# Separate places for the casts and subtractions of the sums and of w_down's parts in the seven-product scheme

## The chip, the cores and the metric

The kernel runs on one core of one Trainium2 chip. The metric is the device time of one execution in microseconds (us). The kernel before takes 2257.21 us, the median of three runs (2255.51 to 2260.72).

## What is computed

The reference is one layer of a streaming encoder on 2048 prompt rows and 64 sample rows of 1024 features. The change lies in its last part, the feed-forward network:

```python
def _post(x, mix, ln1_g, ln1_b, w_gate_up, w_down, ln2_g, ln2_b):
    h = _layernorm(ALPHA * x + mix, ln1_g, ln1_b)
    gu = h @ w_gate_up
    f = (jax.nn.silu(gu[..., :D_FF]) * gu[..., D_FF:]) @ w_down
    return _layernorm(ALPHA * h + f, ln2_g, ln2_b)
```

D_FF is 2816, so w_down is 2816 x 1024. All values are fp32. A matrix product is made of three fp32r products: each operand is held as a high part (a cast) and a low part (the operand minus its high part), and high by high, high by low and low by high are summed in PSUM.

## The kernel before, in words

The rows are worked on in four blocks b (576, 512, 512 and 512 rows). Within a block the 2816 columns of the gate and up matrices come in 22 slices i of 128. The two matrices of a slice are multiplied with the block's h by a scheme of seven smaller products (`product`, numbered 1 to 7), each 12 matmuls of 256 columns in blocks 1 to 3. The list `order` is the order of all these products: for slice i it is 1, then 4 and 3 of the slice before, then 5, 6, 2, 7. So a slice takes seven places of the list and a pair of slices c = (2c, 2c+1) takes 14.

For w_down, blocks 1 to 3 use a second scheme of seven products on most pairs: c = 2 to 9 in blocks 1 and 2, c = 2 to 8 in block 3, 23 pairs in all (`strassen`). One product of a pair is two units (`unit`, u = 0 and 1), each three matmuls of 512 columns (lines 1321 to 1323) into a PSUM bank and one addition by VectorE (DVE) of the bank to y (line 1326). The left operands are g, the gated activations, or sums and differences of g; the right ones are parts of w_down, or differences that were stored in DRAM as wt_d.

The order around the change is written by hand. The last loop goes through `order`; at each place it records first the weights' forms for five places later (`make`), then the product, then what `at(place, ...)` has put there, in the order in which it was put. p0 is the place of product 3 of slice 2c+1; "place n" below means p0 + n, and place 14 is place 0 of the next pair. Each engine does its own instructions strictly in the recorded order. At place 0 the second half of g of the pair's second slice is ready (line 917). Then `put_f` splits it (ScalarE, ACT, casts at line 112; DVE subtracts at line 113), and `f_sums` makes four sums on GpSimd (POOL, line 879) and splits each, all at place 0. The units stand at places 0 to 13; product 2's two units (places 1 and 3) both use bank S0, so the unit at place 3 needs the addition of the one at place 1.

The parts of w_down are loaded (`load_f`, DMA from the SP queue, three buffers "draw"), and split two to six places later by `split_f` (ACT line 112, DVE line 113, five buffers "wd"). POOL, besides, makes the low part of the gate weights' forms 1 and 2 (line 113, wf), each after an ACT cast.

Of the kernel before, what the change touches and what calls it, by code (L numbers as in the profile page):

```python
# [8 lines left out]
F32 = mybir.dt.float32  # L9
F32R = mybir.dt.float32r  # L10
AF = mybir.ActivationFunctionType
ALU = mybir.AluOpType
# [4 lines left out]
P = 128  # L17
# [28 lines left out]
def hybrid_step(ctx: ExitStack, tc: tile.TileContext, x_prompt, x_sample, xT_prompt, xT_sample, cache_kT, cache_v, w_in,  # L46
                ln_v_g, ln_v_b, sinks, w_spatialT, vecs, w_out, w_gate_up, w_down, ln2_g, ln2_b, rope,
                y_prompt, y_sample, wk_p, wv_p, nk_s, nv_s, nvm_s):
    nc = tc.nc
# [61 lines left out]
    def split(hi, lo, src, on=None):  # L111
        nc.scalar.copy(hi, src)  # L112
        (on or nc.vector).tensor_tensor(out=lo, in0=src, in1=hi.bitcast(F32), op=ALU.subtract)  # L113
# [727 lines left out]
            nc.gpsimd.tensor_tensor(out=src, in0=gu_src[b, i][2], in1=src, op=ALU.subtract)  # L841

    ff, acc, part, banks = {}, {}, {}, {}
    ffs, spare, g_t = {}, [], {}

    def bank(name):

# [4 lines left out]
    def half_form():  # L852

        if not spare:
            f = f2.tile([P, 4 * NHX], F32R, name="ff", tag="ff", bufs=4)
            spare.extend(f[:, j * 2 * NHX:j * 2 * NHX + 512].rearrange("p (s t) -> p s t", s=2) for j in range(2))
        return spare.pop(0)
# [12 lines left out]
    def put_f(b, c, prod, src):  # L870
        f = ffs[b, c, prod] = half_form()
        split(f[:, 0], f[:, 1], src)

    def f_sums(b, c):

        x, y = g_t.pop((b, 2 * c)), g_t.pop((b, 2 * c + 1))
        for prod, o, a, d, op in ((5, y[:, 1], x[:, 1], y[:, 1], ALU.add), (7, x[:, 1], x[:, 0], x[:, 1], ALU.subtract),
                                  (6, x[:, 0], y[:, 1], x[:, 0], ALU.subtract), (3, y[:, 0], y[:, 0], x[:, 0], ALU.subtract)):
            nc.gpsimd.tensor_tensor(out=o, in0=a, in1=d, op=op)  # L879
        for prod, o in ((5, y[:, 1]), (6, x[:, 0]), (7, x[:, 1]), (3, y[:, 0])):  # L880
            put_f(b, c, prod, o)

    def tmp(name):
        if early:
# [366 lines left out]
    f2 = fl.enter_context(tc.tile_pool(name="f2", bufs=1, side="right"))  # L1251
# [56 lines left out]
                          w_down[(2 * c + x[0]) * P:(2 * c + x[0] + 1) * P, x[1] * 512:(x[1] + 1) * 512])  # L1308
        d_raw[b, c, "f", prod] = raw

    def split_f(b, c, prod):
        hl = f2.tile([P, 2, 512], F32R, name="wd", tag="wd", bufs=5)
        split(hl[:, 0], hl[:, 1], d_raw.pop((b, c, "f", prod)))
        wd[b, c, "f", prod] = hl

    def unit(b, c, prod, u):
        pd = bank({1: f"D{u}", 6: f"D{u}", 7: f"D{u}", 4: f"D{u}", 2: "S0"}.get(prod, f"S{1 - u}"))
        f, w = ffs[b, c, prod], wd[b, c, "f", prod]
        new = prod in (1, 2, 5)
        fh, fl = f[:, 0, u * P:u * P + P], f[:, 1, u * P:u * P + P]  # L1320
        nc.tensor.matmul(pd, fh, w[:, 0], start=new, stop=False, skip_group_check=not new)  # L1321
        nc.tensor.matmul(pd, fh, w[:, 1], start=False, stop=False, skip_group_check=not new)
        nc.tensor.matmul(pd, fl, w[:, 0], start=False, stop=True, skip_group_check=not new)  # L1323
        r, h = Y_OF[prod]
        y = y_t[TILES[b][2 * r + u]][:, h * 512:(h + 1) * 512]
        nc.vector.tensor_tensor(out=y, in0=pd, in1=y, op=ALU.add)  # L1326
# [104 lines left out]
    def at(pos, f):  # L1431
        todo.setdefault(pos, []).append(f)
# [8 lines left out]
    for b in range(NB):  # L1441
        first, last = b * NO, b == NB - 1
        for c in range(NFF // 2):
            p0 = start[b, 2 * c + 1, 3]
            d_load, d_split = (-8, -1, -5, -3), (-3, 5, -1, 4)
            if strassen(b, 2 * c):
                for prod, q0, q1 in ((1, -7, -3), (2, -6, -2), (6, -2, 2), (5, -1, 3), (3, 1, 5), (7, 3, 7), (4, 5, 9)):
                    at(p0 + q0, lambda b=b, c=c, prod=prod: load_f(b, c, prod))
                    at(p0 + q1, lambda b=b, c=c, prod=prod: split_f(b, c, prod))
                for q, prod, u in ((0, 1, 0), (1, 2, 0), (2, 1, 1), (3, 2, 1), (5, 6, 0), (6, 5, 0), (7, 5, 1), (8, 3, 0), (8, 6, 1),  # L1450
                                   (9, 3, 1), (10, 7, 0), (11, 7, 1), (12, 4, 0), (13, 4, 1)):
                    at(p0 + q, lambda b=b, c=c, prod=prod, u=u: unit(b, c, prod, u))
                continue
            if b == 0:
                d_load, d_split = (-6, -2, 8, 0), (1, 0, 10, 3)
                for j, q0, q1 in ((0, 2, 4), (1, 4, 6), (2, 5, 7), (3, 11, 13)):
                    at(p0 + q0, lambda c=c, j=j: w_sum(c, j))
                    at(p0 + q1, lambda c=c, j=j: w_store(c, j))
            elif c == 0:
                d_load, d_split = (-5, 1, -3, 2), (0, 6, 3, 7)  # L1460
            elif c == 1:
                d_load, d_split = (-8, -1, -4, 1), (-3, 5, 1, 6)
            elif c == NFF // 2 - 1 and not last:
                d_load, d_split = (0, 2, 1, 6), (5, 7, 6, 9)
            elif last and c == NFF // 2 - 2:
                d_load, d_split = (-7, -5, -6, -2), (-4, -2, -3, 2)
            if last and c == NFF // 2 - 1:
                d_load, d_split = (-14, -11, -13, -8), (-11, -3, -4, -2)
            for h in range(2):
                for i in (2 * c, 2 * c + 1):  # L1470
                    at(p0 + d_load[2 * (i % 2) + h], lambda b=b, i=i, h=h: load_d(b, i, h))
                    at(p0 + d_split[2 * (i % 2) + h], lambda b=b, i=i, h=h: split_d(b, i, h, b == NB - 1 and i > NFF - 3 and (i, h) != (NFF - 2, 0)))
            if c < NFF // 2 - (2 if last else 1):
                where = (5, 6, 7, 8, 9, 12, 13, 14, 15, 16) if b == 0 else (2, 4, 5, 7, 9, 10, 12, 13)
                if c == 0 and b:
                    where = (10, 12, 14, 16, 17, 18, 19, 19) if b == 1 else (6, 10, 12, 14, 15, 16, 17, 18)
                for k, (h, t) in enumerate((h, t) for h in (range(2) if b else (1, 0)) for t in TILES[b]):
                    at(p0 + where[k], lambda b=b, c=c, t=t, h=h: down(b, c, t, h))
            elif not last:
                new = list(TILES[b + 1])  # L1480
                if b:
                    at(p0 + 3, lambda t=new.pop(0): new_y(t))
                late = 0 if b else 2
                for k, t in enumerate(TILES[b]):
                    for h in range(2):
                        at(p0 + 10 + 2 * k + (h if b else 2 - h), lambda b=b, c=c, t=t, h=h: down(b, c, t, h))
                    steps = finish_steps(t)
                    for q, f in zip((11, 12, 13, 15, 17), steps):
                        at(p0 + 2 * k + q + late, f)
                    at(p0 + 2 * k + 20 + late, lambda t=new.pop(0): new_y(t)) if new else None  # L1490
        if not last:
            for pos, f in later_steps(b + 1):
                at(first + NO + pos, f)
# [104 lines left out]
```

## Time and profile before

| | |
|---|---|
| median of 3 runs | 2257.21 us (2255.51 to 2260.72) |
| the profiled execution | 2258.49 us, span 2256.3 us |
| busy: TensorE matmul (PE) | 2111.6 us, 94% |
| busy: DVE | 1613.2 us, 71% |
| busy: ACT | 1001.6 us, 44% |
| busy: POOL | 697.8 us, 31% |
| mean granted TensorE clock | 0.975 |

The share of busy time says which engine is loaded, not what it loses. For that one reads whom PE waited for, and then the instructions in order of time around such a wait. The granted clock is given as a share of full speed: 1.00 is 2.4 GHz, 0.50 is 1.2 GHz.

### The profile page before, as it was taken

The numbers are of one execution on the slowest core, as the hardware profiler recorded it, in microseconds if no ns is written. First come the engines' busy times: TensorE is split into PE (matmuls) and PEld (weight loads), VectorE is DVE, ScalarE is ACT, GpSimd is POOL, SyncE is SP. The second block draws the span as 40 slices with busy tenths as digits, with TensorE's granted clock in tenths as the row PEclk, the third lists the DMA queues.
The fourth block names the chain that finished last, engine by engine and source line by source line (L and its number), as shares of the span: only waits on it lengthen the run. The fifth ranks groups of instructions, "written<-read, shape, count | busy, mean of one in ns | idle before, by whom it ended". The sixth has DMA issues, their size and how long they took to land.

```text
span 2256.3 us, 36282 instructions
## 1 busy us (share of the span) xinstructions
PE 2111.6 (94%) x13081; PEld 1887.1 (84%) x13081; DVE 1613.2 (71%) x3176; ACT 1001.6 (44%) x2385; POOL 697.8 (31%) x644
## 2 busy tenths in 40 slices
PE   8999999989988999999999899999998999999997
PEld 6888888867767899899888888888888888988886
DVE  6877777786887767777785666677576668566665
ACT  6666666653444444444423334343333344334443
POOL 0222222121223667766411332221223212122220
PEclk9999999989999999999999999999999999999999
DMA  5111111144564767767875676777676667766663
GB/s 192 38 38 38 41 50 34 34 144 156 193 215 175 290 230 262 260 246 262 289 268 200 238 268 215 252 276 259 231 248 242 244 236 292 241 223 226 235 232 119
DMA packets 189155, 447.21 MB, mean 198 GB/s; under 512 B 22608, under 2 KB 53072, under 8 KB 188976
## 3 DMA queue, kind: packets, MB, share of 16 engines
q1 hardware_dynamic: 168432, 426.22, 53.8%
q10 hardware_dynamic: 20368, 18.35, 2.4%
q8 instruction: 103, 1.69, 0.3%
q14 instruction: 76, 0.62, 0.1%
q0 software_dynamic: 176, 0.33, 0.1%
HBM read 345.94 MB, written 98.89 MB: 197 GB/s over the span
## 4 chain that ended last, share of the span: by engine, by line
PE 59%; DVE 21%; ACT 6%; issue 5%; POOL 4%; DMA 4%; ACTq 0%; SPq 0%; DVEq 0%; POOLq 0%
PE bankA L900 5%; PE bankA L901 4%; PE bankA L902 4%; POOL g L879 2%; PE pj L158 2%; PE pj L159 2%; PE pj L160 2%; DVE ff L113 2%; PE po L160 2%; PE po L158 2%; PE po L159 2%; DVE y L1326 2%; PE pd L159 2%; PE bankC L901 2%; PE pd L160 2%
## 5 line engine op out<-in xcount | busy, mean ns | idle before, releaser
L113 POOL TENSOR_TENSOR wf<-guraw,wf 128x512 fp32r<-128x512 f32 x173 | 249.5, 1442 | 702.5 <-ACT wf L112 679.8
L900 PE MATMUL bankA<-hf,wf 128*128 128x256 f32 x1056 | 312.7, 296 | 14.9 <-ACT a L906 14.8
L901 PE MATMUL bankA<-hf,wf 128*128 128x256 f32 x1056 | 310.6, 294 | 0.0
L902 PE MATMUL bankA<-hf,wf 128*128 128x256 f32 x1056 | 310.4, 294 | 0.0
L113 DVE TENSOR_TENSOR wd<-draw,wd 128x512 fp32r<-128x512 f32 x245 | 183.1, 748 | 116.2 <-ACT wd L112 113.1
L900 PEld LDWEIGHTS bankA<-hf,wf 128*128 128x128 f32 x1056 | 213.5, 202 | 27.5 <-ACT a L906 18.3
L901 PEld LDWEIGHTS bankA<-hf,wf 128*128 128x128 f32 x1056 | 213.1, 202 | 9.4
L902 PEld LDWEIGHTS bankA<-hf,wf 128*128 128x128 f32 x1056 | 212.7, 201 | 0.0
L112 ACT CAST wf<-guraw 128x512 fp32r<-128x512 f32 x264 | 163.2, 618 | 15.9 <-DMA guraw<-in_w_gate_up_dram 8.7
L906 ACT COPY a<-bankA 128x256 f32<-128x256 f32 x198 | 73.3, 370 | 203.6 <-PE bankA L902 203.3
L901 PE MATMUL bankC<-hf,wf 128*128 128x256 f32 x528 | 149.3, 283 | 2.7 <-DVE hf L113 2.7
L112 ACT CAST wd<-draw 128x512 fp32r<-128x512 f32 x245 | 150.8, 616 | 1.5 <-PE bankD L160 0.8
L900 PE MATMUL bankC<-hf,wf 128*128 128x256 f32 x528 | 149.4, 283 | 0.0
L902 PE MATMUL bankC<-hf,wf 128*128 128x256 f32 x528 | 148.4, 281 | 0.0
L113 DVE TENSOR_TENSOR ff<-g,ff 128x256 fp32r<-128x256 f32 x161 | 80.2, 520 | 86.9 <-ACT ff L112 86.9
L1326 DVE TENSOR_TENSOR y<-bankD,y 128x512 f32<-128x512 f32 x184 | 125.8, 684 | 22.5 <-PE bankD L1323 22.5
L941 ACT ACTIVATE a<-a 128x256 f32<-128x256 f32 (+1 forms) x88 | 37.4, 425 | 226.2 <-DVE a L910 225.1
L112 ACT CAST ff<-g 128x256 fp32r<-128x256 f32 x161 | 63.2, 406 | 163.5 <-DVE g L917 101.2
L900 PE MATMUL accA<-hf,wf 128*128 128x288 f32 x352 | 105.0, 298 | 8.5 <-ACT a L906 4.9
L1321 PE MATMUL bankS<-wd,ff 128*128 128x512 f32 x138 | 58.4, 423 | 58.1 <-DVE y L1326 58.1
L901 PEld LDWEIGHTS bankC<-hf,wf 128*128 128x128 f32 x528 | 99.5, 188 | 8.7 <-DVE hf L113 3.2
L902 PE MATMUL accA<-hf,wf 128*128 128x288 f32 x352 | 104.0, 296 | 0.4 <-DVE wf L113 0.4
(332 smaller groups left out, 6592.1 us busy)
## 6 DMA issues: line engine op xcount, KB each, us to landing
wf<-wf_d SPq DMA_DIRECT2D x264, 512.0 KB, 5.1
guraw<-in_w_gate_up_dram SPq DMA_DIRECT2D x110, 512.0 KB, 6.2
wf_d<-wf SPq DMA_DIRECT2D x88, 512.0 KB, 4.8
draw<-in_w_down_dram SPq DMA_DIRECT2D x153, 256.0 KB, 4.0
draw<-wt_d SPq DMA_DIRECT2D x92, 256.0 KB, 5.5
guraw<-in_w_gate_up_dram SPq DMA_DIRECT2D x66, 256.0 KB, 6.5
wt_d<-draw SPq DMA_DIRECT2D x44, 256.0 KB, 3.3
hraw<-h_d SPq DMA_DIRECT2D x42, 256.0 KB, 5.7
```

The costliest lines, as they stand in the source:

```text
L112: nc.scalar.copy(hi, src)
L113: (on or nc.vector).tensor_tensor(out=lo, in0=src, in1=hi.bitcast(F32), op=ALU.subtract)
L158: nc.tensor.matmul(out, ah, bh, start=(i == 0), stop=False)
L159: nc.tensor.matmul(out, ah, bl, start=False, stop=False)
L160: nc.tensor.matmul(out, al, bh, start=False, stop=(i == n - 1))
L879: nc.gpsimd.tensor_tensor(out=o, in0=a, in1=d, op=op)
L900: nc.tensor.matmul(ps, wh, hh, start=(new and k == 0), stop=False, skip_group_check=not new)
L901: nc.tensor.matmul(ps, wh, hl, start=False, stop=False, skip_group_check=not new)
L902: nc.tensor.matmul(ps, wl, hh, start=False, stop=(k == 3), skip_group_check=not new)
L906: nc.scalar.copy(part[i, key][:, :n], ps)
L1321: nc.tensor.matmul(pd, fh, w[:, 0], start=new, stop=False, skip_group_check=not new)
L1326: nc.vector.tensor_tensor(out=y, in0=pd, in1=y, op=ALU.add)
```

## The change

Three things change for the 23 pairs. `f_sums` keeps the four sums on POOL at place 0, but their casts and subtractions are no longer made there: for the sums of products 5, 6, 3 and 7 the cast (`put_hi`) is at places 3, 4, 5, 6 and the subtraction (`put_lo`) one place later. The split of w_down's parts becomes a cast (`split_hi`) and, one place later, a subtraction (`split_lo`). Products 5 and 6 change places (the units at 5 and 6), with their loads and splits, and four of the loads are one place later.

```diff
+            f_sum[b, c, prod] = o
-            put_f(b, c, prod, o)
+    def put_hi(b, c, prod):
+        ffs[b, c, prod] = half_form()
+        nc.scalar.copy(ffs[b, c, prod][:, 0], f_sum[b, c, prod])
+    def put_lo(b, c, prod):
+        f = ffs[b, c, prod]
+        nc.vector.tensor_tensor(out=f[:, 1], in0=f_sum.pop((b, c, prod)), in1=f[:, 0].bitcast(F32), op=ALU.subtract)
...
-                for prod, q0, q1 in ((1, -7, -3), (2, -6, -2), (6, -2, 2), (5, -1, 3), (3, 1, 5), (7, 3, 7), (4, 5, 9)):
+                for prod, q0, q1 in ((1, -6, -3), (2, -5, -2), (5, -2, 2), (6, -1, 3), (3, 1, 5), (7, 4, 7), (4, 6, 9)):
                     at(p0 + q0, lambda b=b, c=c, prod=prod: load_f(b, c, prod))
-                    at(p0 + q1, lambda b=b, c=c, prod=prod: split_f(b, c, prod))
+                    at(p0 + q1, lambda b=b, c=c, prod=prod: split_hi(b, c, prod))
+                    at(p0 + q1 + 1, lambda b=b, c=c, prod=prod: split_lo(b, c, prod))
...
+                for q, prod in ((3, 5), (4, 6), (5, 3), (6, 7)):
+                    at(p0 + q, lambda b=b, c=c, prod=prod: put_hi(b, c, prod))
+                    at(p0 + q + 1, lambda b=b, c=c, prod=prod: put_lo(b, c, prod))
```

What stands in a row on DVE around place 0, before. The names: a is a partial result of a gate product, g the gated activations and their sums, ff the split form of either, wf a form of the gate weights, wd the split part of w_down, y the output rows; bankS_12902 is bank S0.

```order
L910 TENSOR_TENSOR a_14932<-bankC_12337,a_14932 128x256
L917 TENSOR_TENSOR g<-a_14979,a_14932 128x256
L113 TENSOR_TENSOR ff<-g,ff 128x256 x5
L1326 TENSOR_TENSOR y<-bankD_12798,y 128x512
L113 TENSOR_TENSOR wf<-guraw,wf 128x512
L1326 TENSOR_TENSOR y<-bankS_12902,y 128x512
L113 TENSOR_TENSOR wd<-draw,wd 128x512
L1326 TENSOR_TENSOR y<-bankD_12852,y 128x512
L910 TENSOR_TENSOR a_15004<-bankS_12228,a_15004 128x256
```

The same stretch on DVE after the change, from place 0 to the subtraction of product 5's sum at place 4 and the first addition of product 5 (bankS_12228 is bank S1):

```order
L926 TENSOR_TENSOR g<-a_14979,a_14930 128x256
L113 TENSOR_TENSOR ff<-g,ff 128x256
L1338 TENSOR_TENSOR y<-bankD_12798,y 128x512
L113 TENSOR_TENSOR wf<-guraw,wf 128x512
L1338 TENSOR_TENSOR y<-bankS_12902,y 128x512
L1338 TENSOR_TENSOR y<-bankD_12852,y 128x512
L919 TENSOR_TENSOR a_15003<-bankS_12228,a_15003 128x256
L1326 TENSOR_TENSOR wd<-draw,wd 128x512
L1338 TENSOR_TENSOR y<-bankS_12902,y 128x512
L946 TENSOR_TENSOR a_15154<-bankC_12168,a_15154 128x256
L1326 TENSOR_TENSOR wd<-draw,wd 128x512
L890 TENSOR_TENSOR ff<-g,ff 128x256
```

Four of the five ff subtractions have left the head of this stretch; the first of them now stands at its end, behind line 946 and a wd subtraction.

On ACT, before, at places 0 to 5 of a pair:

```order
L112 CAST ff<-g 128x256 x5
L112 CAST wf<-guraw 128x512
L906 COPY a_14763<-bankA_12134 128x256
L112 CAST wd<-draw 128x512
L941 ACTIVATE a_14654<-a_14654 128x256
L112 CAST wd<-draw 128x512
L906 COPY a_14815<-bankA_12134 128x256
L112 CAST wf<-guraw 128x512
```

On ACT, after, for the same places:

```order
L112 CAST ff<-g 128x256
L112 CAST wf<-guraw 128x512
L915 COPY a_14753<-bankA_12134 128x256
L1322 CAST wd<-draw 128x512
L950 ACTIVATE a_14653<-a_14653 128x256
L1322 CAST wd<-draw 128x512
L886 CAST ff<-g 128x256
L915 COPY a_14803<-bankA_12134 128x256
L886 CAST ff<-g 128x256
L112 CAST wf<-guraw 128x512
```

At place 4 a cast of a sum (line 886) has come between the copy of product 7 (line 915) and the cast of form 2 (line 112), whose low part POOL makes.

## Rows read from the trace of the kernel before

**Rows 1.** PE's waits: what was waited for, us in total, times, longest.
```profile
PE bankS L1321 <- DVE y L1326: 58.1, 25, 5.7
```

**Rows 2.** Stretches: length, each engine's busy time (instructions), granted clock, DMA share, GB/s.
```profile
1213.00:1490.40 277.40, 253.94 (x1681) 235.33 (x1680) 184.23 (x326) 108.65 (x245) 78.97 (x72) 0.94 0.69 240
1592.30:1866.50 274.20, 250.97 (x1682) 232.38 (x1681) 184.43 (x326) 108.75 (x245) 79.04 (x72) 0.96 0.69 242
1968.40:2200.50 232.10, 217.78 (x1472) 202.61 (x1471) 151.84 (x282) 93.52 (x212) 60.16 (x56) 0.96 0.65 227
1357.30:1389.40 32.10, 30.05 (x213) 27.92 (x211) 21.54 (x41) 13.38 (x30) 8.61 (x9) 1.00 0.69 237
1389.40:1423.00 33.60, 31.56 (x213) 29.31 (x211) 21.54 (x40) 13.29 (x30) 8.59 (x9) 0.95 0.65 228
1479.50:1484.00 4.50, 3.30 (x22) 2.69 (x21) 4.50 (x7) 1.41 (x3) 0.89 (x1) 1.00 0.41 106
```

**Rows 3.** Timeline at places 0 to 3 of a pair: start, us, instruction [idle before <-releaser].
```profile
1391.40 0.43 DVE L113 TENSOR_TENSOR ff<-g,ff 128x256 fp32r<-128x256 f32 x1 [0.47 <-ACT ff L112]
...
1391.91 3.27 POOL L879 TENSOR_TENSOR g<-g 128x256 f32<-128x256 f32 x4 [1.69 <-DVE ff L113]
...
1394.83 1.30 DVE L113 TENSOR_TENSOR ff<-g,ff 128x256 fp32r<-128x256 f32 x3 [1.08 <-ACT ff L112]
...
1396.05 0.68 DVE L1326 TENSOR_TENSOR y<-bankD,y 128x512 f32<-128x512 f32 x1
...
1396.65 0.68 DVE L113 TENSOR_TENSOR wf<-guraw,wf 128x512 fp32r<-128x512 f32 x1
1397.25 0.68 DVE L1326 TENSOR_TENSOR y<-bankS,y 128x512 f32<-128x512 f32 x1
...
1397.98 0.50 PE L1321 MATMUL bankS<-wd,ff 128*128 128x512 f32 x1 [2.04 <-DVE y L1326]
```

**Rows 4.** Timeline at places 11 and 12 of the same pair, around product 7's end.
```profile
1416.62 0.39 PE L1321 MATMUL bankD<-wd,ff 128*128 128x512 f32 x1
...
1416.82 0.37 ACT L906 COPY a<-bankA 128x256 f32<-128x256 f32 x1 [1.25 <-PE bankA L902]
...
1417.09 0.40 PE L1323 MATMUL bankD<-wd,ff 128*128 128x512 f32 x1
...
1417.09 0.62 ACT L112 CAST wd<-draw 128x512 fp32r<-128x512 f32 x1
...
1417.23 0.42 DVE L937 TENSOR_TENSOR a<-bankC,a 128x256 f32<-128x256 f32 x1 [1.15 <-ACT a L906]
...
1417.57 0.68 DVE L1326 TENSOR_TENSOR y<-bankD,y 128x512 f32<-128x512 f32 x1
...
1417.61 0.62 ACT L112 CAST wf<-guraw 128x512 fp32r<-128x512 f32 x1
...
1418.16 0.68 DVE L113 TENSOR_TENSOR wd<-draw,wd 128x512 fp32r<-128x512 f32 x1
...
1418.31 1.69 POOL L113 TENSOR_TENSOR wf<-guraw,wf 128x512 fp32r<-128x512 f32 x1 [10.08 <-ACT wf L112]
...
1418.74 0.40 PE L1321 MATMUL bankD<-wd,ff 128*128 128x512 f32 x1
```

**Rows 5.** Timeline where ACT casts a sum and then a form (place 13).
```profile
1387.93 0.41 ACT L112 CAST ff<-g 128x256 fp32r<-128x256 f32 x1 [1.69 <-DVE g L917]
1388.24 0.62 ACT L112 CAST wf<-guraw 128x512 fp32r<-128x512 f32 x1
```

**Rows 6.** Timeline where DVE and POOL both read SBUF.
```profile
1269.72 1.48 POOL L747 TENSOR_TENSOR hraw<-hraw,hsum 128x512 f32<-128x512 f32 x1
...
1269.97 1.78 DVE L113 TENSOR_TENSOR wd<-draw,wd 128x512 fp32r<-128x512 f32 x1
```

**Rows 7.** A unit's last matmul and its weight load: duration ns min/median/max, span, form.
```profile
L1323 PEld LDWEIGHTS bankD<-wd,ff x184: 187/187/188, 1214.6 to 2200.0; 128*128 128x128 f32 x184
```

**Rows 8.** Loads of w_down's parts (line 1307): time from issue to landing.
```profile
DMA to landing us min/median/max: 2.5/4.3/8.8
```

More of the change, by code (lines that the diff above doesn't have):

```diff
@@ L843, in hybrid_step @@
     ff, acc, part, banks = {}, {}, {}, {}
-    ffs, spare, g_t = {}, [], {}
+    ffs, spare, g_t, f_sum = {}, [], {}, {}
     def bank(name):
@@ L1309, in load_f, with split_hi, split_lo @@
         d_raw[b, c, "f", prod] = raw
[L1311 to L1314, printed above, removed]
+    def split_hi(b, c, prod):
+        hl = wd[b, c, "f", prod] = f2.tile([P, 2, 512], F32R, name="wd", tag="wd", bufs=5)
+        nc.scalar.copy(hl[:, 0], d_raw[b, c, "f", prod])
+    def split_lo(b, c, prod):
+        hl = wd[b, c, "f", prod]
+        nc.vector.tensor_tensor(out=hl[:, 1], in0=d_raw.pop((b, c, "f", prod)), in1=hl[:, 0].bitcast(F32), op=ALU.subtract)
     def unit(b, c, prod, u):
@@ L1446, in hybrid_step @@
             if strassen(b, 2 * c):
-                for prod, q0, q1 in ((1, -7, -3), (2, -6, -2), (6, -2, 2), (5, -1, 3), (3, 1, 5), (7, 3, 7), (4, 5, 9)):
+                for prod, q0, q1 in ((1, -6, -3), (2, -5, -2), (5, -2, 2), (6, -1, 3), (3, 1, 5), (7, 4, 7), (4, 6, 9)):
                     at(p0 + q0, lambda b=b, c=c, prod=prod: load_f(b, c, prod))
-                    at(p0 + q1, lambda b=b, c=c, prod=prod: split_f(b, c, prod))
-                for q, prod, u in ((0, 1, 0), (1, 2, 0), (2, 1, 1), (3, 2, 1), (5, 6, 0), (6, 5, 0), (7, 5, 1), (8, 3, 0), (8, 6, 1),
+                    at(p0 + q1, lambda b=b, c=c, prod=prod: split_hi(b, c, prod))
+                    at(p0 + q1 + 1, lambda b=b, c=c, prod=prod: split_lo(b, c, prod))
+                for q, prod, u in ((0, 1, 0), (1, 2, 0), (2, 1, 1), (3, 2, 1), (5, 5, 0), (6, 6, 0), (7, 5, 1), (8, 3, 0), (8, 6, 1),
                                    (9, 3, 1), (10, 7, 0), (11, 7, 1), (12, 4, 0), (13, 4, 1)):
                     at(p0 + q, lambda b=b, c=c, prod=prod, u=u: unit(b, c, prod, u))
+                for q, prod in ((3, 5), (4, 6), (5, 3), (6, 7)):
+                    at(p0 + q, lambda b=b, c=c, prod=prod: put_hi(b, c, prod))
+                    at(p0 + q + 1, lambda b=b, c=c, prod=prod: put_lo(b, c, prod))
                 continue
```

## The prediction

> **What bounds the kernel now.** PE is busy nearly all the time, so I first read whom it waited for. One row stands out: a unit into bank S waited for DVE's addition to y, 58.1 us in 25 waits [rows 1]. The second view is the table of stretches [rows 2]. Its first three rows are the three stretches with the 23 pairs of the seven-product scheme, 277.4 + 274.2 + 232.1 = 783.7 us. A place with one unit takes 2.12 us, from one unit's start to the next (1416.62 to 1418.74) [rows 4], so a pair without waits would take 14 x 2.12 = 29.7 us and 23 of them 683 us. About 101 us are lost there. The table also shows the granted clock at 0.94, 0.96 and 0.96 in these stretches: some of the time is spent at 1.2 GHz instead of 2.4, which costs 277.4 x 0.06 + 274.2 x 0.04 + 232.1 x 0.04 = 37 us. A pair whose clock stayed at 1.00 takes 32.1 us, one with a drop 33.6 (fourth and fifth row) [rows 2]: 2.4 us of waiting, and 1.5 us more where the clock fell.
>
> The third view, the order of time at places 0 to 3, says where the wait comes from [rows 3]. DVE subtracts the first ff at 1391.40. It then stands at the head of four more, each of which needs an ACT cast of a sum that POOL is still making (four sums, 3.27 us from 1391.91). The last three end at 1396.13. Behind them are queued two additions to y and one weight subtraction; the addition from bank S0, whose unit had long ended, starts only at 1397.25 and ends at 1397.93, and PE, after 2.04 us of idling, starts the unit of place 3 at 1397.98.
>
> **Part one, the sums' splits leave place 0.** No instruction is removed or added; 23 x 4 casts and 23 x 4 subtractions move. DVE's queue at place 0 is then the ff subtraction (2.00 us after the unit of place 0 starts, at 1389.40), an addition, a weight subtraction and the addition from S0. With the spacing of 0.60 us from one 512-wide operation to the next [rows 3] they start at 2.34, 2.94 and 3.54 and the last ends at 4.2. The unit of place 3 is due at 3 x 2.13 = 6.4. Even if the weight subtraction, now beside POOL's sums, takes 1.78 us as one does beside POOL [rows 6], the addition ends at 5.4. So this wait goes, and with it the drop of the clock that follows. Worth: 58.1 us of waits plus 37 us of clock, 95 us, less 3 us that I leave off, because two of the 25 waits must be at other places (there are 23 pairs) and because the half clock costs nothing where it falls into a wait: 92 us. The stretches' lengths allow 101 at most.
>
> **Part two, the first subtraction that is now due late.** What is late next? I walked the new order from place 0 with the rows' spacings, looking for each unit at when its operands are ready. One place comes out short: the third matmul of product 5's first unit (place 5), which needs the subtraction put at place 4. Count from the end of product 7 (place 4), as which the end of the same product at 1416.62 can stand [rows 4]. ACT's copy starts at 0.20 and DVE's addition of line 937 at 0.61. The next DVE instruction starts 0.34 later, at 0.95; it is now a wd subtraction. The ff subtraction stands behind it, 0.60 later, at 1.55, and takes 0.43 [rows 3]: 1.98. PE meanwhile does product 1, 1.42 us (1417.32 to 1418.74 at this spot, a place less a unit of 0.70), and two matmuls, 0.47 (1416.62 to 1417.09) [rows 4]: the third is due at 1.89, and its weights must be loaded first (0.19 us) [rows 7]. Undisturbed, that is a wait of about 0.3 us a pair.
>
> But POOL is there at the same moment. After the copy ACT's next cast starts 0.27 later, at 0.47 [rows 4]; it is now a sum's cast, and the form's cast follows 0.31 later [rows 5], at 0.78, takes 0.62, and POOL starts 0.08 after its end (1418.23 to 1418.31) [rows 4], at 1.48. What two engines reading SBUF do to each other can be seen [rows 6]: a wd subtraction of 0.68 us that started 0.25 us after a POOL subtraction took 1.78, ending 0.55 us after POOL's end; it was held until POOL was done. The other way round POOL's subtraction came 0.15 us after a DVE one and took 1.69 us where the one on its own takes 1.29 (1.69 less the 0.40 for which DVE held it) [rows 4]. So DVE's wd subtraction holds POOL until about 0.95 + 0.55 = 1.50, POOL gets its turn there, before the ff subtraction at 1.55, and keeps it until 2.79; the ff subtraction then needs some 0.28 more, as its 0.43 less the start-up that passes while it is held, and ends at 3.07. With 0.05 for the signal (1397.93 to 1397.98) [rows 3] and the weight load the third matmul starts at 3.3 instead of 1.89: 1.4 us a pair, 32 us in 23 pairs. The margin is thin, 0.05 to 0.07 us, between POOL's 1.48 to 1.50 and DVE's 1.55; I take the collision, because in all my sums POOL comes first, and keep the other end, 7 us, for the range.
>
> **Part three, w_down's casts and subtractions a place apart.** DVE no longer stands waiting for ACT between the two. That time is off PE's path once part one has emptied the queue; I cost it at nothing, and the later subtraction of each part (half a place to a place before its unit) has at least 1 us in hand in my walk, but for bank S1 at place 10, where the addition of product 3's unit ends only some 0.2 us before product 2 needs the bank. If that fails it costs tenths of a us. The loads of four parts have three places, 6.4 us, instead of four until their cast; the median landing is 4.3 us, the longest 8.8 [rows 8]. The loads are issued as soon as their buffer is free, mostly 7 us or more before the cast by my walk; I cost this at nothing too. The exchange of products 5 and 6 moves equal work.
>
> **Sum.** 2258.5 - 92 + 32 = 2198.5 us for the profiled execution, and 1.3 less on the scale of the median, 2197 us.
>
> **The rivals.** First, DVE gets its ff subtraction in before POOL: 2258.5 - 92 + 7, or 2172 us on the median's scale. For it: the margin is under 0.1 us, and a form's cast that waits for its DMA comes later. Against: every spacing above is a row's, and they repeat to 0.01 us.
>
> Second, the new waits of 1.4 us also pull the clock down, at 1.5 us each: up to 23 x 1.5 = 35 us, 2231 us if in every pair, 2214 if in half. Against it: in the last row PE waits about 1.2 us in 4.5 and the clock is 1.00; and even the 2.4 us wait left it at 1.00 in the pair of the fourth row [rows 2]. The Trainium skill speaks for it (TensorE: Matmul & The Clock Gate, "A second HAM failure mode: psum-queue depth-cycling"): an engine that idles briefly but often between groups of matmuls is reported to swing between its two clocks. By that rule I would have the 2231 us; the trace so far does not agree, since the row at 1479.5 shows such an idle at 1.00.
>
> Third, slower than before: the loads. ACT works in order, so a w_down part that lands after its cast's turn holds the copies of lines 906 behind it, and PE stops at bank A. From a loss of 92 / 23 = 4.0 us a pair on the kernel is slower; two of the four loads with a window cut by a place would each have to come 2 us late. At 6.4 us or more against a median of 4.3 that takes landings near the longest in every pair; with 4.4 us a pair it would be 2257 + 9 = 2266 us.
>
> Fourth, the change doesn't free DVE: the wd and wf subtractions beside POOL's sums keep the S0 addition late. It has 1 us in hand at the worst [rows 6], so that takes two such delays in a row: then the time stays near 2257.
>
> **How the numbers follow.** The forecast has 0.52, the first rival 0.24, the second 0.15 (2210 to 2231), the slower one 0.05, no change 0.04. The range takes in the forecast, the first rival and the lower part of the second: 2166 (the first rival with half of the 9 us that lie between 92 and 101) to 2218. A measurement of this kernel tells 0.2%, about 4.5 us, from no change. Faster by more than that: 0.52 + 0.24 + 0.15 and a little of the fourth, 0.92; within: 0.03; slower: 0.05.
>
> **What would show it.** PE's wait for line 1326 at the unit of place 3 should be gone, and the clock in the three stretches at 0.99 or 1.00. In its place PE's weight load, or the matmul, of the third line of a unit into bank S should wait for the ff subtraction (line 890), 23 times some 1.4 us, and the POOL subtraction of form 2 should overlap it there. If that ff subtraction takes 0.43 us instead of about 1.5, the first rival is right. If the clock still falls in most pairs, the second. If ACT waits for draw, the third. If the S0 addition is still late, part one is wrong.

## The result and the profile after

The changed kernel takes 2207.3 us (median of 4 runs, 2203.86 to 2207.81) against 2256.36 us for the kernel before, measured beside it (4 runs, 2254.44 to 2260.72): a ratio of 0.9777, 95% interval 0.9759 to 0.9794. It is faster by 49 us; I had forecast 60, and a range that holds the time. The profiled execution took 2207.18 us, its span is 2205.4 us. One run of one kernel further down (2295.36 us, at a mean granted clock of 0.845 against 0.99 in its other three) is left out of that kernel's time.

Line numbers are those of each kernel. In the kernel after and in the edits of it, a unit's matmuls are lines 1333 to 1335 (1321 to 1323 before), the addition to y is line 1338 (1326 before), line 1326 is now the wd subtraction, line 890 the ff subtraction of a sum, and 909 to 911 are a gate product's matmuls.

First, whom PE waited for in the kernel after (line, what was waited for, us in total, times, longest), to be read beside [rows 1]:

```profile
PE bankS L1335 <- DVE ff L890: 25.3, 23, 2.2
...
PE bankS L909 <- DVE y L1338: 7.7, 6, 2.3
```

The wait for the addition at the first matmul of a unit, 58.1 us in 25 waits before, is gone from the head of the list. In its place stand 23 waits, one in each pair, of the third matmul of a unit for a subtraction of line 890: part two of the prediction. The second row shows something else, six waits of product 2 for bank S1. To it I come below.

Second, the stretches that answer to [rows 2]: the three stretches with the 23 pairs, then an ordinary pair, then the fourth (I count the pairs from 1 to 23 in order of time; length, busy time of each engine, granted clock, DMA share, GB/s):

```profile
1214.30:1472.70 258.40, 243.70 (x1671) 223.26 (x1670) 192.28 (x327) 106.85 (x244) 79.30 (x72) 0.99 0.75 261
1574.90:1828.10 253.20, 241.07 (x1670) 221.88 (x1670) 191.80 (x325) 107.18 (x244) 79.09 (x72) 0.99 0.76 265
1932.00:2149.10 217.10, 209.19 (x1462) 192.88 (x1461) 163.30 (x281) 91.88 (x211) 58.45 (x56) 1.00 0.69 241
1277.10:1308.20 31.10, 30.05 (x212) 27.76 (x211) 23.36 (x42) 12.57 (x29) 8.05 (x8) 1.00 0.76 265
1308.20:1345.50 37.30, 32.57 (x213) 29.16 (x212) 24.78 (x42) 13.72 (x31) 15.09 (x13) 0.95 0.68 247
```

The clock is at 0.99 to 1.00 where it was at 0.94 to 0.96. An ordinary pair takes 31.1 us instead of 32.1 or 33.6. Taken in both traces from the start of the first unit's first matmul to the end of the last unit (0.23 us, the step from one of its matmuls to the next, after the start of its last one), the stretches have 276.0 + 272.8 + 230.6 = 779.4 us before and 258.3 + 253.2 + 217.0 = 728.5 after: 50.9 us less, which is the whole change of the span (2256.3 to 2205.4).

Third, the order of time at places 0 to 3 of an ordinary pair, against [rows 3]. The unit of place 0 starts at 1994.16:

```profile
1993.70 1.29 POOL L113 TENSOR_TENSOR wf<-guraw,wf 128x512 fp32r<-128x512 f32 x1 [2.93 <-ACT wf L112]
1994.07 1.46 DVE L1326 TENSOR_TENSOR wd<-draw,wd 128x512 fp32r<-128x512 f32 x1
...
1997.25 0.43 DVE L113 TENSOR_TENSOR ff<-g,ff 128x256 fp32r<-128x256 f32 x1 [0.47 <-ACT ff L112]
...
1997.76 3.52 POOL L879 TENSOR_TENSOR g<-g 128x256 f32<-128x256 f32 x4 [2.77 <-DVE ff L113]
1998.19 0.85 DVE L113 TENSOR_TENSOR wf<-guraw,wf 128x512 fp32r<-128x512 f32 x1
...
1998.97 0.68 DVE L1338 TENSOR_TENSOR y<-bankS,y 128x512 f32<-128x512 f32 x1
...
2000.54 0.40 PE L1333 MATMUL bankS<-wd,ff 128*128 128x512 f32 x1
```

DVE no longer stands behind POOL's sums. The addition out of bank S0 ends at 1999.65, 0.9 us before the unit of place 3, which starts on time, 6.38 us after the unit of place 0. One row I had not foreseen: the wd subtraction at 1994.07, now a place later than before, meets POOL's form and takes 1.46 us, and the first ff subtraction starts 3.09 us after the unit of place 0 instead of 2.00. Here that lies in front of nothing; later experiments show what it costs without that cover.

Fourth, places 4 and 5 of the same pair:

```profile
2003.27 0.42 DVE L946 TENSOR_TENSOR a<-bankC,a 128x256 f32<-128x256 f32 x1 [0.84 <-ACT a L915]
...
2003.61 0.68 DVE L1326 TENSOR_TENSOR wd<-draw,wd 128x512 fp32r<-128x512 f32 x1
...
2004.14 1.29 POOL L113 TENSOR_TENSOR wf<-guraw,wf 128x512 fp32r<-128x512 f32 x1 [2.86 <-ACT wf L112]
2004.21 1.50 DVE L890 TENSOR_TENSOR ff<-g,ff 128x256 fp32r<-128x256 f32 x1
...
2005.77 0.50 PE L1335 MATMUL bankS<-wd,ff 128*128 128x512 f32 x1 [1.05 <-DVE ff L890]
```

This is the collision of part two. POOL starts 0.07 us before the ff subtraction (I had 0.05 to 0.07), the ff subtraction takes 1.50 us instead of 0.43 and ends 0.28 us after POOL, and the third matmul waits for it.

### The profile page after: what moved, and what is told of

It is laid out like the page before. It is cut to its first block, busy times and chain, and to the rows that moved or that the text cites. A ratio compares the mean times of both kernels' runs of the same rounds, so it can differ in the third digit from the quotient of the medians.

```text
span 2205.4 us, 36220 instructions
## 1 busy us (share of the span) xinstructions
PE 2089.7 (95%) x13081; PEld 1861.6 (84%) x13081; DVE 1640.3 (74%) x3176; ACT 997.0 (45%) x2385; POOL 702.2 (32%) x644
## 4 chain that ended last, share of the span: by engine, by line
PE 65%; DVE 20%; ACT 6%; DMA 4%; issue 3%; POOL 1%; ACTq 0%; SPq 0%; DVEq 0%; POOLq 0%
PE bankA L909 5%; PE bankA L911 4%; PE bankA L910 4%; PE pj L158 2%; PE pj L159 2%; PE pj L160 2%; PE bankC L910 2%; PE bankC L909 2%; PE bankC L911 2%; PE pd L159 2%; PE pd L160 2%; PE pd L158 2%; PE bankD L1334 2%; PE bankD L1333 2%; PE bankD L1335 2%
## 5 line engine op out<-in xcount | busy, mean ns | idle before, releaser
L909 PE MATMUL bankA<-hf,wf 128*128 128x256 f32 x1056 | 301.8, 286 | 12.2 <-ACT a L915 11.9
L910 PE MATMUL bankA<-hf,wf 128*128 128x256 f32 x1056 | 300.1, 284 | 0.0
L911 PE MATMUL bankA<-hf,wf 128*128 128x256 f32 x1056 | 299.9, 284 | 0.0
L909 PEld LDWEIGHTS bankA<-hf,wf 128*128 128x128 f32 x1056 | 201.4, 191 | 22.7 <-ACT a L915 14.6
L910 PEld LDWEIGHTS bankA<-hf,wf 128*128 128x128 f32 x1056 | 201.2, 191 | 9.1
L911 PEld LDWEIGHTS bankA<-hf,wf 128*128 128x128 f32 x1056 | 201.4, 191 | 0.0
L1326 DVE TENSOR_TENSOR wd<-draw,wd 128x512 fp32r<-128x512 f32 x161 | 130.8, 813 | 0.0
L950 ACT ACTIVATE a<-a 128x256 f32<-128x256 f32 (+1 forms) x88 | 37.4, 425 | 200.7 <-DVE a L919 199.7
L909 PE MATMUL accA<-hf,wf 128*128 128x288 f32 x352 | 105.2, 299 | 8.9 <-ACT a L915 5.3
L958 ACT ACTIVATE a<-a 128x256 f32<-128x256 f32 (+1 forms) x88 | 37.4, 424 | 155.9 <-DVE a L919 155.8
L910 PEld LDWEIGHTS bankC<-hf,wf 128*128 128x128 f32 x528 | 99.5, 188 | 8.6 <-DVE hf L113 3.2
L1338 DVE TENSOR_TENSOR y<-bankS,y 128x512 f32<-128x512 f32 x138 | 94.4, 684 | 16.1 <-PE bankS L1335 13.7
L909 PEld LDWEIGHTS bankC<-hf,wf 128*128 128x128 f32 x528 | 99.8, 189 | 7.0 <-DMA wf<-wf_d 1.4
L911 PE MATMUL accA<-hf,wf 128*128 128x288 f32 x352 | 104.1, 296 | 0.4 <-DVE wf L113 0.4
L910 PE MATMUL accA<-hf,wf 128*128 128x288 f32 x352 | 104.4, 297 | 0.0
```

Source lines behind the costliest of these rows:

```text
L909: nc.tensor.matmul(ps, wh, hh, start=(new and k == 0), stop=False, skip_group_check=not new)
L910: nc.tensor.matmul(ps, wh, hl, start=False, stop=False, skip_group_check=not new)
L911: nc.tensor.matmul(ps, wl, hh, start=False, stop=(k == 3), skip_group_check=not new)
L1326: nc.vector.tensor_tensor(out=hl[:, 1], in0=d_raw.pop((b, c, "f", prod)), in1=hl[:, 0].bitcast(F32), op=ALU.subtract)
```

## The experiments

Times of the changed kernel and of the edits are medians of 4 runs, of 3 or 10 where it is said; the kernel before, run beside each group, lay at 2257.3 to 2260.4 us. Where less than 1% matters, I compare the three stretches of the traces, taken as above; each trace is one execution, and the runs of one kernel lie up to 6 us apart. Every edit is against the changed kernel unless it says otherwise.

**The ff subtraction ahead of the wd subtraction.**

```diff
-                    at(p0 + q1 + 1, lambda b=b, c=c, prod=prod: split_lo(b, c, prod))
+                    if prod != 6:
+                        at(p0 + q1 + 1, lambda b=b, c=c, prod=prod: split_lo(b, c, prod))
...
+                at(p0 + 4, lambda b=b, c=c: split_lo(b, c, 6))
```

> From the changed kernel, one line moved: at place 4 the ff subtraction of product 5's sum is recorded ahead of the wd subtraction of product 6, so that on DVE it stands directly behind the addition into a. My theory (the ff subtraction is late because it stands behind the wd one, and POOL's form-2 subtraction slips in between): the ff subtraction takes about 0.4 us, PE's wait of 1.3 us at the third matmul of product 5's first unit goes in all 23 pairs, an ordinary pair takes 29.8 us instead of 31.1, and the time is 2207 - 30 = 2177 us, give or take 5. The rival (the wait hides another one that ends just behind it, on the weight half or the bank): a pair stays at 30.5 us or more and the time at 2195 or above.

Measured: 2180.26 us, ratio to before 0.9654 (0.9638 to 0.967); the stretches are 29.7 us shorter than in the changed kernel. DVE and POOL at place 4 of an ordinary pair:

```profile
1981.76 0.42 DVE L890 TENSOR_TENSOR ff<-g,ff 128x256 fp32r<-128x256 f32 x1
1982.09 0.68 DVE L1326 TENSOR_TENSOR wd<-draw,wd 128x512 fp32r<-128x512 f32 x1
...
1982.28 1.64 POOL L113 TENSOR_TENSOR wf<-guraw,wf 128x512 fp32r<-128x512 f32 x1 [2.85 <-ACT wf L112]
```

Nobody holds the ff subtraction now (0.42 us), the row of 23 waits shrinks to one of 0.5 us, and an ordinary pair takes 29.8 us. POOL takes 1.64 us instead of 1.29, and nobody waits for that. The theory holds.

**Only POOL later.** DVE's order stays; a cast on ACT is put in front of that of form 2.

```diff
-                for q, prod in ((3, 5), (4, 6), (5, 3), (6, 7)):
-                    at(p0 + q, lambda b=b, c=c, prod=prod: put_hi(b, c, prod))
-                    at(p0 + q + 1, lambda b=b, c=c, prod=prod: put_lo(b, c, prod))
+                for q0, q1, prod in ((3, 4, 5), (4, 5, 6), (4, 6, 3), (6, 7, 7)):
+                    at(p0 + q0, lambda b=b, c=c, prod=prod: put_hi(b, c, prod))
+                    at(p0 + q1, lambda b=b, c=c, prod=prod: put_lo(b, c, prod))
```

> From the changed kernel, one cast moved: ACT casts product 3's sum at place 4 instead of 5, ahead of the cast of the gate weights' form 2, so that POOL's low part of that form becomes ready about 0.3 us later; DVE's order is untouched. My theory (POOL gets in ahead of the ff subtraction by less than 0.1 us and holds it): the ff subtraction now comes first and takes 0.43 us instead of 1.5, PE's wait at product 5 shrinks from 1.3 to about 0.3 us, and the time falls by 23 x 1.0 = 23 us to 2184, give or take 6. The rival (the ff subtraction is late by DVE's own queue and POOL has no part in it): ff keeps its 1.5 us or the wait its 1.3 us, and the time stays at 2207 +- 4.

Measured: 2186.71 us, ratio 0.968 (0.9666 to 0.9695).

```profile
2019.75 0.68 DVE L1326 TENSOR_TENSOR wd<-draw,wd 128x512 fp32r<-128x512 f32 x1
2020.35 0.42 DVE L890 TENSOR_TENSOR ff<-g,ff 128x256 fp32r<-128x256 f32 x1
...
2020.59 1.34 POOL L113 TENSOR_TENSOR wf<-guraw,wf 128x512 fp32r<-128x512 f32 x1 [3.16 <-ACT wf L112]
```

POOL comes 0.24 us after the ff subtraction instead of 0.07 before it, the ff subtraction takes 0.42 us with the wd subtraction still ahead of it, and the distance from the unit of place 5 to that of place 6 is 2.35 us instead of 3.46 (2.13 without a wait). So of the 1.3 us of a pair, 1.1 are POOL's and 0.2 DVE's own queue.

**Cast and subtraction of w_down together again (part three undone alone).**

```diff
-                    at(p0 + q1 + 1, lambda b=b, c=c, prod=prod: split_lo(b, c, prod))
+                    at(p0 + q1, lambda b=b, c=c, prod=prod: split_lo(b, c, prod))
```

> From the changed kernel, part three undone alone: cast and subtraction of each w_down part are put at one place again (that of the cast). My theory (the place apart is worth nothing by itself; what matters is who stands ahead of the ff subtraction at place 4): the wd subtraction of product 6 moves ahead of place 4's addition, the ff subtraction of product 5 comes directly behind that addition, the wait at product 5 goes, and a shorter wait of about 0.5 us comes up at product 6; time 2185 us, give or take 8. The rival (the place's lead keeps DVE from standing behind ACT's casts, and is part of the gain): DVE waits for casts of wd and the time is 2207 us or more.

Measured: 2206.94 us, ratio 0.9769 (0.9755 to 0.9784), no different from the changed kernel. I had forecast 22 us less. DVE and POOL at place 4:

```profile
2063.63 0.69 DVE L1326 TENSOR_TENSOR wd<-draw,wd 128x512 fp32r<-128x512 f32 x1 [0.99 <-ACT wd L1322]
2064.24 0.69 DVE L1338 TENSOR_TENSOR y<-bankS,y 128x512 f32<-128x512 f32 x1
2064.84 0.42 DVE L946 TENSOR_TENSOR a<-bankC,a 128x256 f32<-128x256 f32 x1
...
2065.11 1.27 POOL L113 TENSOR_TENSOR wf<-guraw,wf 128x512 fp32r<-128x512 f32 x1 [3.96 <-ACT wf L112]
2065.17 1.50 DVE L890 TENSOR_TENSOR ff<-g,ff 128x256 fp32r<-128x256 f32 x1
```

As I thought, the ff subtraction stands directly behind the addition of line 946. But the wd subtraction waited 0.99 us for its cast, the addition behind it came 0.6 us late, and so POOL again comes first, by 0.06 us. A place between cast and subtraction is thus worth something on DVE; the changed order spends it by putting a wd subtraction in the way. The next run tests this.

**The same, and POOL later.** The last edit and the one before it together.

> From the kernel with cast and subtraction of w_down at one place again (2207 us), one cast moved: product 3's sum is cast at place 4 instead of 5, ahead of the cast of form 2, so that POOL's subtraction is ready 0.3 us later. In that kernel the ff subtraction stands directly behind the addition into a, and still took 1.50 us, because POOL started at 2065.11 and it at 2065.17, in a typical pair. My theory (a race for one port, lost by 0.06 us): ff now comes first and takes 0.43 us, the wait at product 5 falls from 1.3 to about 0.3 us, and the time by 23 us to 2184, give or take 7. The rival (DVE's later addition into a makes the wait by itself): 2200 us or more.

Measured: 2197.36 us (median of 3 runs), ratio 0.973 (0.9714 to 0.9746): less of a gain than the 2184 us that I expected. The order at places 4 and 5, and one row of PE's waits:

```profile
2058.03 0.41 DVE L890 TENSOR_TENSOR ff<-g,ff 128x256 fp32r<-128x256 f32 x1
2059.04 1.09 DVE L1326 TENSOR_TENSOR wd<-draw,wd 128x512 fp32r<-128x512 f32 x1 [0.60 <-ACT wd L1322]
```

```profile
PE bankD L1335 <- DVE ff L890: 8.7, 23, 1.5
```

The race is won, as expected (0.41 us), and the distance at place 5 falls to 2.36 us. But now the next wd subtraction, behind its cast, meets POOL and takes 1.09 us, product 6's ff subtraction comes late, and the distance at place 6 is 2.61 instead of 2.13 us. 1.1 us less and 0.5 us more in 23 pairs are 13 us; the stretches are 11.5 us shorter than in the run before it. This second wait I had written into the expectation of the run before, and left out here.

**The sums' splits at place 0 again (part one undone alone).**

```diff
-            f_sum[b, c, prod] = o
+            put_f(b, c, prod, o)
...
-                for q, prod in ((3, 5), (4, 6), (5, 3), (6, 7)):
-                    at(p0 + q, lambda b=b, c=c, prod=prod: put_hi(b, c, prod))
-                    at(p0 + q + 1, lambda b=b, c=c, prod=prod: put_lo(b, c, prod))
```

> From the changed kernel, part one undone alone: the four sums are split at place 0 again, directly behind POOL's sums; the w_down parts keep their separate places, and products 5 and 6 their exchange. My theory (the splits at place 0 alone made the wait for bank S0 at place 3 and the drops of the clock): the wait is back with about 2.2 us a pair, the clock in the three stretches at 0.94 to 0.96, and the wait at product 5 is gone; the time is 2250 us, give or take 6. The rival (w_down's new places carry a part of the gain of 49 us): 2240 us or less.

Measured: 2287.81 us, ratio 1.0128 (1.0113 to 1.0143): the old wait is back, and the kernel is 29 us slower than before the change, where I expected 8 less than before. One row of PE's waits, and the order at places 0 to 3 (the unit of place 0 at 2058.77):

```profile
PE bankS L1333 <- DVE y L1338: 77.1, 23, 5.7
```

```profile
2058.31 1.29 POOL L113 TENSOR_TENSOR wf<-guraw,wf 128x512 fp32r<-128x512 f32 x1 [2.93 <-ACT wf L112]
...
2058.69 1.46 DVE L1326 TENSOR_TENSOR wd<-draw,wd 128x512 fp32r<-128x512 f32 x1
2060.07 0.41 DVE L919 TENSOR_TENSOR a<-bankC,a 128x256 f32<-128x256 f32 x1
...
2065.28 1.29 DVE L113 TENSOR_TENSOR ff<-g,ff 128x256 fp32r<-128x256 f32 x3 [1.07 <-ACT ff L112]
```

It is the row at 1994.07 again: product 2's wd subtraction, moved by part three into the way of POOL's form. In the trace of before the addition of line 910 that answers to the one of line 919 starts 0.20 us after the unit of place 0, here 1.30, and everything behind it (g, POOL's sums, the five ff subtractions) is 1.1 us later too. 23 x 1.1 = 25 us, and the clock falls behind this wait in 21 pairs instead of 18.

**The same, with product 2's wd subtraction back at its old place.** Against the last kernel:

```diff
-                    at(p0 + q1 + 1, lambda b=b, c=c, prod=prod: split_lo(b, c, prod))
+                    at(p0 + q1 + (prod != 2), lambda b=b, c=c, prod=prod: split_lo(b, c, prod))
```

> From the kernel with the sums split at place 0 again (2288 us), one more thing undone: the low part of w_down for product 2 is made at place -2, with its cast, as before the change, instead of at -1. My theory for the 30 us by which that kernel is slower than the one before the change: at place -1 this subtraction starts 0.37 us after POOL's form-1 subtraction, takes 1.46 us instead of 0.68, and pushes g, POOL's sums and the five subtractions behind them back by 1.09 us, and the clock falls in more pairs. Without it the wait at place 3 is 2.2 us again instead of 3.3, and the time 2258 us, give or take 8. The rival (the other w_down places or the exchange of products 5 and 6 make the 30 us): 2275 us or more.

Measured: 2255.33 us (median of 10 runs), ratio to before 0.999 (0.998 to 1.0). The one subtraction accounts for all of the 30 us. The run says more: this kernel still has the exchange of products 5 and 6, the later loads and six of the seven parts' separate places, and is at the time of before. With the sums at place 0 these together are worth nothing, one way or the other.

**The same subtraction moved in the changed kernel.** The edit of the last run, made on the changed kernel.

> From the changed kernel, only the low part of w_down for product 2 at place -2 again. With the sums split at place 0 this edit alone was worth 32 us (2288 to 2255). My theory (with the splits gone from place 0, the 1.1 us by which g comes earlier are in front of nothing): 2207 us, give or take 4. The rival (the delay still reaches PE, by the sums or by the bank): 2200 us or less.

Measured: 2206.19 us, ratio 0.976 (0.9744 to 0.9776): no more than the runs differ among themselves. An ordinary pair takes 31.1 us in both. The stretches of its trace are 4.2 us shorter, 3.3 of them in the fourth pair alone, but that trace is of the fastest of its four runs (2203.34 us). So with the splits away from place 0 the 1.1 us are covered by the time in hand of the bank S0 addition.

This kernel and that of the run before it (2255.33 us) differ by part one alone: by 49 us in their times, by 52 against the kernel before that ran beside each. That is all that the whole change brought.

**Product 7's wd subtraction a place later.**

```diff
-                    at(p0 + q1 + 1, lambda b=b, c=c, prod=prod: split_lo(b, c, prod))
+                    at(p0 + q1 + (2 if prod == 7 else 1), lambda b=b, c=c, prod=prod: split_lo(b, c, prod))
```

> From the changed kernel, one subtraction moved: the low part of w_down for product 7 is made at place 9 instead of 8, so that on DVE the addition of product 3's unit out of bank S1 no longer stands behind it. My theory (the 7.7 us that PE waits for bank S1 at place 10, and the drops of the clock that follow, make most of what the four slow pairs lose beyond an ordinary one): the waits at place 10 shrink to 2 us or less in all, and the three stretches together get 5 to 9 us shorter; time about 2200 us. The rival (the additions in those pairs are late for work that stands ahead of both, h's preparation on DVE and ACT): the stretches stay within 2 us and the time at 2207.

The edit aims at the second row of the first view. In the eighth pair of the changed kernel, where DVE also splits the next block's h (line 113, hf), the order at places 8 to 10 reads

```profile
1459.40 0.69 DVE L113 TENSOR_TENSOR hf<-hraw,hf 128x512 fp32r<-128x512 f32 x1
...
1459.73 1.48 POOL L113 TENSOR_TENSOR wf<-guraw,wf 128x512 fp32r<-128x512 f32 x1 [9.68 <-ACT wf L112]
...
1460.00 1.76 DVE L1326 TENSOR_TENSOR wd<-draw,wd 128x512 fp32r<-128x512 f32 x1
1461.68 0.68 DVE L1338 TENSOR_TENSOR y<-bankS,y 128x512 f32<-128x512 f32 x1
...
1462.42 0.38 PE L909 MATMUL bankS<-hf,wf 128*128 128x256 f32 x1 [2.25 <-DVE y L1338]
```

The wd subtraction meets POOL (1.76 us), the addition out of bank S1 stands behind it, and PE loses 2.25 us for the bank. Behind that the clock falls, as the stretch around it shows (the first 0.79 is the granted clock):

```profile
1460.00:1466.00 6.00, 3.75 (x18) 3.29 (x18) 5.39 (x9) 1.90 (x5) 1.21 (x1) 0.79 0.79 259
```

Measured with the edit: 2203.53 us, ratio 0.976 (0.9746 to 0.9775), the stretches 6.5 us shorter. The row of bank S1 falls from 7.7 us to 2.6, not quite to the 2 us I had set. The eighth and the sixteenth pair take 3.0 and 1.5 us less, the second, the tenth and the last 0.6; the fourth and the twelfth stay at 37.0 and 33.7 us. So of the four slow pairs the theory holds for the eighth and the sixteenth, not for the fourth and the twelfth.

**The second half of h's preparation four places later.**

```diff
-            q = -100 + 24 * kk
+            q = -100 + 28 * kk
```

> From the changed kernel, one number: the second half of the preparation of the next block's h (loads, sums on POOL, splits) starts 28 places after the first instead of 24, that is at the same places of a pair as the first half. My theory (pairs 4 and 12 lose 6.1 and 2.7 us because POOL's work on h at places 0 to 6 of these pairs delays the sums' subtractions and the weights behind them): these losses fall to those of pairs 2 and 10, 0.6 us, and the time by 6 to 8 us to 2200. The rival (it is the store of h on the queue of the weights' loads, wherever it stands): the loss only moves to another pair, and the time stays at 2207 +- 3.

Measured: 2202.2 us, ratio 0.9752 (0.9738 to 0.9767), the stretches 6.1 us shorter. In the changed kernel the fourth pair takes 37.3 us (last row of the second view); POOL's work for h stands there at places 0 to 6:

```profile
1316.59 1.29 POOL L747 TENSOR_TENSOR hsum<-hraw 128x512 f32<-128x512 f32 x1
1317.96 1.60 POOL L747 TENSOR_TENSOR hsum<-hraw,hsum 128x512 f32<-128x512 f32 x1
1319.52 1.46 POOL L747 TENSOR_TENSOR hraw<-hraw 128x512 f32<-128x512 f32 x1
1320.94 1.29 POOL L113 TENSOR_TENSOR wf<-guraw,wf 128x512 fp32r<-128x512 f32 x1
```

In the twelfth pair (33.7 us) the same work meets place 4:

```profile
1678.18 1.27 POOL L747 TENSOR_TENSOR hraw<-hraw 128x512 f32<-128x512 f32 x1
1678.20 1.81 DVE L1326 TENSOR_TENSOR wd<-draw,wd 128x512 fp32r<-128x512 f32 x1
...
1679.42 1.70 POOL L113 TENSOR_TENSOR wf<-guraw,wf 128x512 fp32r<-128x512 f32 x1
...
1679.93 1.48 DVE L890 TENSOR_TENSOR ff<-g,ff 128x256 fp32r<-128x256 f32 x1
...
1681.46 0.50 PE L1335 MATMUL bankS<-wd,ff 128*128 128x512 f32 x1 [2.16 <-DVE ff L890]
```

The wd subtraction comes behind POOL's work for h (1.81 us) and the ff subtraction behind POOL's form, so PE waits 2.16 us instead of 1.05 for product 5, and the clock falls behind it (0.72):

```profile
1681.00:1687.00 6.00, 5.54 (x29) 5.26 (x30) 3.44 (x8) 1.64 (x4) 1.55 (x2) 0.72 1.02 413
```

With the edit the fourth and the twelfth pair take 31.7 us each, 0.6 above an ordinary one; the sixteenth rose by 1.4.

**The three together, and with product 2's subtraction back as well.** First the edits of the ff order, of product 7 and of h in one kernel:

> From the changed kernel, the three edits together that each took time off: the ff subtraction of product 5 ahead of the wd one (2207 to 2180 us), product 7's low part at place 9 (to 2203.5), the second half of h's preparation at 28 places from the first (to 2202). If they act on separate waits, as I think, the gains add: 27 + 4 + 5 = 36 us, 2171 us, and the losses beyond an ordinary pair of 29.8 us are under 4 us in the three stretches. The rival (with the wait at product 5 gone, the edits at place 9 and at h meet other work and take from each other): 2176 us or more.

Then that kernel with product 2's wd subtraction at place -2:

> The last kernel, and the low part of w_down for product 2 at place -2 again, so that it doesn't meet POOL at place -1 and g is ready 1.1 us earlier. My theory (in this order the 1.1 us lie in front of nothing, since the addition from bank S0 has over 1 us in hand): within 2 us of the kernel without this edit, about 2171 us. The rival (an earlier g gives the pairs with other work room): 3 us or more faster.

Measured: 2165.12 us, ratio 0.958 (0.9565 to 0.9594), and 2165.23 us, ratio 0.9579 (0.9565 to 0.9594). The first beats both kernels of this case; the second shows again that the early subtraction is worth nothing here. The three stretches and what is left of the bank S1 row in the first of them:

```profile
1216.20:1454.20 238.00, 237.42 (x1671) 221.12 (x1670) 180.88 (x325) 106.88 (x244) 82.20 (x72) 1.00 0.79 279
1558.20:1796.10 237.90, 237.33 (x1670) 221.04 (x1669) 180.63 (x325) 107.03 (x244) 82.05 (x72) 1.00 0.79 279
1899.40:2106.60 207.20, 207.20 (x1460) 193.37 (x1459) 154.85 (x280) 91.93 (x210) 60.88 (x56) 1.00 0.71 250
```

```profile
PE bankS L909 <- DVE y L1338: 1.1, 2, 0.6
```

The stretches have 238.0 + 237.9 + 207.2 = 683.1 us and PE is busy in 682 of them. The edits gave 42 us where the single ones had 36 in the medians. In the stretches, which leave out the rest of the program, it is 45.4 against 29.7 + 6.5 + 6.1 = 42.3 us: the gains add, with 3 us more, as they would if they act on separate waits.

## Why the prediction was right, and what it missed

Against the 683 us that the stretches take without waits, the kernel before lost 779.4 - 683 = 96.4 us and the one after loses 728.5 - 683 = 45.5.

**Part one was right.** The wait for the bank S0 addition at place 3 is gone from the pairs, and with it the drops of the clock behind it, which came in 18 of 23 pairs before and in none after. My walk had the addition end 4.2 us after the unit of place 0, and 5.4 at the worst; it ended at 5.5 (1.1 us of the delay is the late g of part three), so its time in hand was 0.9 us and not 2.2. Undoing the part alone brought the wait back, and the two kernels that differ by it alone are 49 us apart (2255.33 and 2206.19).

**Part two was right in its place, cause and size.** Place, line and number of waits are as forecast, and but for the twelfth pair the wait costs 3.46 - 2.13 = 1.3 us a pair, 30 us, where I had 1.4 and 32. The bold step was to decide a margin of 0.05 to 0.07 us for POOL. The trace shows POOL 0.07 us ahead in 21 pairs; a sum of some ten spacings came out that well, which was not sure, and I had given the other side 0.24. The runs with POOL later and with ff first show that this margin, and no second wait behind it, is the term: 21 and 27 us faster.

**Part three was wrong in its reason, right in its sum.** I said that a place between cast and subtraction costs nothing because the queue is empty. In fact product 2's subtraction was moved into the way of POOL's form-1 subtraction and delays g by 1.1 us a pair. In the changed order that is covered (2206.19 against 2207.3 us without it); with the sums' splits at place 0 it cost 32 us (2287.81 against 2255.33). Had the change been made without part one, my nothing would have been an error of 32 us. The exchange of products 5 and 6 was not tried alone; with the sums split at place 0 it, the later loads and six parts' separate places together cost nothing.

**The term that was mis-sized is the rest.** My sum, 96.4 - 92 + 32 = 36.4 us of loss, left 4.4 us for everything outside an ordinary pair. The trace has 45.5 - 30.1 = 15.4. These 11 us, less the 2 by which the place 5 term was too high, are the 9.1 by which the stretches' 50.9 us fall short of the 60 forecast (49 in the medians). The step that failed is the walk of one typical pair, counted 23 times, and in it the sentence on bank S1 at place 10: I saw that only 0.2 us were in hand there and wrote that a failure costs tenths of a us. In pairs in which POOL and DVE also prepare the next block's h, PE waits there 2.3 us in the sixteenth, 2.25 in the eighth, where the clock falls behind it, 1.9 in the fourth and 0.4 in the second and the tenth. The edit at product 7's subtraction took 6.5 us from the stretches, nearly all of it in the second, eighth, tenth, sixteenth and last pair. The fourth and the twelfth, 6.1 and 2.7 us above an ordinary pair, lose theirs where POOL's work for h stands, the twelfth at product 5: the edit of h took 7.5 us from these two and gave 1.4 back in the sixteenth. With the ff order as well, nearly all of the rest went (683.1 us). The trace of before could have warned me: there the second, third, fourth, tenth and twelfth pair take 35.7 to 37.9 us, against 33.6 for a pair with a drop of the clock. Which of the steps in the fourth pair (the sums' subtractions behind POOL's work, the weight loads behind h's store) makes most of its 6.1 us stays open: the edit of h moves both, and with product 2's subtraction back alone the pair took 33.9 us in the trace instead of 37.2, for which no run here shows the reason.

**The rivals.** The first, DVE first, is what the second experiment made, with 2187 us; I had 2172 for it, mostly because the same 11 us of other losses were missing. (The low end of my range, 2166, should be some 2168 by its own working; nothing hangs on it.) The second, a clock that falls at the new waits, did not come: 22 of the 23 waits, with some 1.1 us of idling each, were not followed by a drop, and in the ordinary pairs it stayed at 1.00. The rule of the Trainium skill by which I gave it a chance (TensorE: Matmul & The Clock Gate, "A second HAM failure mode: psum-queue depth-cycling") is not borne out here. The clock did fall behind single longer waits, such as the 2.25 us at bank S1 in the eighth pair and the 2.16 at product 5 in the twelfth. The third: w_down's parts landed at a median of 3.7 us (longest 9.6) against 4.3 and 8.8 in [rows 8], and ACT waited for them 8.7 us in 4 waits, no more. (In the 23 pairs a part is split four places after its load, not two to six, and after the change three places for the four loads that moved.) The fourth was wrong too: the unit of place 3 came 2.12 or 2.13 us after that of place 2 in all 23 pairs.

## What to carry to other kernels

When a hand-written order is changed, walk not only the ordinary period but also those in which some other work shares the queues; a place with 0.2 us in hand is one that can fail there. Where two engines want to read SBUF within 0.1 us of each other, write down who comes first and what waits for the loser: swapping two neighbours in a queue gave 27 us here, more than half of what the whole change brought. A move that costs nothing does so only under a cover, and the cover should be named, because the next edit may take it away.

## What the runs showed of the hardware that I had not expected

- The margin of such a race can be 0.06 us, and it repeats: in the changed kernel it is 0.07 us in 21 of the 23 pairs (0.39 and 0.51 in the fourth and the twelfth, with POOL's work for h): with POOL 0.06 or 0.07 us ahead the ff subtraction took 1.50 us, with POOL 0.24 us behind it 0.42.
- The loss of the two is not the same. The DVE subtraction that came second was held until POOL was done (1.50 us instead of 0.42); the POOL subtraction that came 0.19 us after a 512-wide DVE one took 1.64 us instead of 1.29, and one that came 0.53 us after such a start was not held at all (1.29).
- Holding shows as busy time. The 161 wd subtractions of the 23 pairs take 813 ns in the mean after the change, against 0.68 us for one alone. In the whole program the ff subtractions of g and its sums are busy for 104.2 us instead of 80.2 and the wd ones for 196.9 instead of 183.1, and DVE for 1640.3 us instead of 1613.2, with as many instructions. A rise of the busy time without more work is worth a look at who else reads at that moment.
